# Gated convolution's input with five block groups and four plain tiles, on unscaled operands, and ACT and DVE in a held order at its head

## The chip, the cores and the metric

The kernel runs on one core of a Trainium2 chip. The metric is the time of one execution on the device in microseconds (us); lower is better. The core's engines are PE (TensorE, matmuls), DVE (VectorE), ACT (ScalarE), POOL (GpSimd) and SP (SyncE); SP and POOL here mostly issue DMAs.

## The reference

A causal decoder trunk of two layers over 512 tokens of width 1024, all in float32. Layer 0 is an attention mixer followed by a gated MLP, layer 1 a gated short convolution followed by another gated MLP. The part that is changed is the first half of layer 1's mixer:

```python
def rms_norm(x, g):
    xf = x.astype(jnp.float32)
    y = xf * lax.rsqrt(jnp.mean(xf * xf, axis=-1, keepdims=True) + EPS)
    return (y * g.astype(jnp.float32)).astype(x.dtype)

def short_conv_mixer(h, norm_g, w_in, conv_w, w_out):
    xn = rms_norm(h, norm_g)
    proj = xn @ w_in
    gate_b = proj[..., :CONV_WIDTH]
    gate_c = proj[..., CONV_WIDTH:2 * CONV_WIDTH]
    u = proj[..., 2 * CONV_WIDTH:]
    y = gate_b * causal_dwconv(gate_c * u, conv_w)
    return y @ w_out
```

`causal_dwconv` is a depthwise convolution over three tokens; `CONV_WIDTH` is 1024, so `proj` has 3072 columns: three parts of eight tiles of 128.

## The kernel before

Activations lie transposed, features on the partitions and the 512 tokens along the row, so the residual `h` is eight tiles of 128x512. TensorE works in a reduced form of float32; every operand is kept as a high half and a low half, and a product of two operands is three matmuls: high by high, low by high, high by low. For weights, the high half `whi` is a rounding copy by ACT, and the low half `wlo` is the difference, by DVE.

A matrix product is done in one of two ways:

- A **plain tile** is 128 output columns by all 512 tokens: 8 blocks of features, three matmuls each, 24 matmuls of 512 columns (`products`, `mm3`, L336 to L338). Its weights come through a list (`want`, `weights`) with `whi` at L315 and `wlo` at L316. The operands are `hs_a` and `hs_b`, the halves of `h` times the norm's gain. They are not scaled by the norm's factor of the token, which comes later and is multiplied onto the result.
- A **block group** (class `Sevens`) is 256 output columns by all 512 tokens, computed as a 2x2 block product (features in two halves, tokens in two halves) with seven products in place of eight. Each product is 24 matmuls of 256 columns (`seven`, L1078). They run in the order p1, p7, p3, p6, p2, q5, q4, one in each slot (`slot(g, s)`), where the slot of p3 does that of the group before. Each product has an operand form, made once for all groups out of the blocks of the operand (a, b the left and right tokens of the first four feature tiles, c, d those of the last four), and weights made for each group: four blocks X, Y, W, Z by DMA, sums of them by accumulating DMAs on POOL's queue (`add_block`) and by DVE (`Y+=X`, L1144; `Y+=W`, L1199), and halves by ACT and DVE (`weights_of`, L1027 and L1029). PSUM bank A gathers p1 and p2, bank T p7 and q4, bank R p3, p6 and q5. R begins as a copy of −A that ACT makes in slot 1 (L1185), and p6 of the same group accumulates into it.

`halves_to` makes a form's halves: `p7_hi` by ACT, then `p7_lo` by DVE.

The gated convolution's input has 24 tiles of output columns. Before, eight are plain (u and gate_c tiles 0 and 1, then gate_b tiles 0 to 3), and sixteen are block groups 1 to 4: groups 1 to 3 hold u and gate_c tiles 2g and 2g+1, group 4 gate_b tiles 4 to 7. The groups' operand is scaled: `prepare` multiplies `h` by gain and norm row into `x0` and `x1` (eight rows of 128x512 on DVE, L1453), then makes the seven forms. The pieces of `prepare`, and of the scaling and convolution of the plain tiles (`input_`, `gate`), are chores that `up.work_off(SHARE)` hands out between the matmuls of the plain tiles.

The norm's factor `norm.row` is made late: squares of `h` (`sq_n`, ACT), sums on PE (L410), thirteen small rows of 128x4 on DVE, a turn on PE (L396), and a copy on ACT (L397). `norm.finish(x)` sets when, and `norm.scaled(f)` puts off `f` until the row is there.

The order of instructions on an engine is the scheduler's, save where the code holds it: `pin(m)` and `behind(m, n)` hold single instructions, and with `strict[0]` set ACT and DVE keep the order in which the code is written. `tail(p, s)` does the elementwise work of a group once its results are there: u times gate_c, the convolution, times gate_b, and the halves `y` for the output product, which begins after the last group (L336 and so on into bank `psa`).

Of the kernel before, what the change touches and what calls it, by code (L numbers as in the profile page):

```python
# [17 lines left out]
F32 = mybir.dt.float32  # L18
# [7 lines left out]
P = 128  # L26
# [24 lines left out]
FAR = 41  # L51
CHUNKS = ((2, 3), (5, 3), (8, 3)), ((0, 3), (3, 4), (7, 4))
EARLY, LATER = 4.0, 5.0
SHARE = 0.58


@with_exitstack
def trunk(
# [967 lines left out]
    def halves_to(hi, lo, src, sign=1.0, held=()):  # L1026
        made = act.activation(hi, src, AF.Copy, scale=sign)  # L1027
        if sign > 0:
            rest = dve.tensor_tensor(lo, src, f32(hi), op=ALU.subtract)  # L1029
        else:  # L1030
            rest = dve.scalar_tensor_tensor(lo, src, -1.0, f32(hi), op0=ALU.mult, op1=ALU.subtract)
        for m, engine in ((made, "act"), (rest, "dve")):
            if engine in held:
                pin(m)

    LEFT, RIGHT = slice(0, HT), slice(HT, S)
    FORMS = ("p1", "p7", "p3", "p6", "p2", "q5", "q4")
# [45 lines left out]
    class Sevens:  # L1083
# [23 lines left out]
        def weights_of(self, g, form, n):  # L1107
            hi, lo = (wp.tile([P, CHUNK], F32R, tag=f"w{t}", name=f"w{t}_{form}{self.name}{g}", bufs=3)[:, 0:1024].rearrange(
                "p (k c) -> p k c", c=2 * P) for t in ("hi", "lo"))
            halves_to(hi, lo, self.st[g][n], held=("act",))  # L1110
            self.st[g][form] = hi, lo

        def bank_of(self, g, n):
# [16 lines left out]

        def join(self, g, n, acc, other):
            to = self.wides[g][n][:, :, RIGHT]
            dve.tensor_tensor(to, acc.rearrange("p (i t) -> p i t", t=HT), other.rearrange("p (i t) -> p i t", t=HT), op=ALU.subtract)
            if self.scaled:
                dve.tensor_tensor(to, to, self.row(RIGHT), op=ALU.mult)

# [231 lines left out]
    def conv_seven(norm, mp, rp):  # L1368

        def block_of(g, kh, half):  # L1370
            c0 = (4 + 2 * half) * P if g == 4 else (2 - half) * D + 2 * g * P
            return conv_w_in[0][kh * 512:(kh + 1) * 512, c0:c0 + 2 * P].rearrange("(k p) c -> p k c", p=P)

        up = Sevens("c", mp, range(1, 5), block_of)
        up.norm, up.chores, up.ahead = norm, [], True
        chores, wides, room = up.chores, up.wides, []

        def eight(dt, name):
            t = rp.tile([P, 8, S], dt, tag="head", name=name)
            return t[:, 0:4, :], t[:, 4:8, :]  # L1380
        early_t, early_b = eight(F32, "early")
        ys = []

        def place(k, n):
            if not room:
                room.append(hsp.tile([P, 12, S], F32, tag="hs_a", name="hs_a_conv"))
            return room[0][:, k:k + n, :]
        up.wides_of = lambda g: {"yg": place(8, 2), "yv": place(10, 2)}

        def conv(o, src):  # L1390
            dst = early_t[:, 2 + o, :] if o < 2 else place(o, 1)[:, 0, :]
            causal_conv(dst, src, lambda i: conv_tap(i, o))

        def halves_in(o, n):
            y_hi, y_lo = ys[o // 4]
            at_ = slice(o % 4, o % 4 + n)
            halves_to(y_hi[:, at_, :], y_lo[:, at_, :], place(o, n))

        def open_ys():
            ys.append((hsp.tile([P, 4, S], F32R, tag="hs_b", name="y_hi1"), rp.tile([P, 4, S], F32R, tag="four", name="y_lo1")) if ys else eight(F32R, "y0"))  # L1400

        def times(o, side, with_):
            t = place(o, 2)[:, :, side]
            dve.tensor_tensor(t, t, with_, op=ALU.mult)

        def by_tile(acc):
            return acc.rearrange("p (i t) -> p i t", t=HT)

        def left(g, acc):
            if g == 4:  # L1410
                times(4, LEFT, by_tile(acc))
            else:
                up.to_wide(g, "yg", LEFT, acc)

        def early(g, acc):
            if g == 4:
                times(6, LEFT, by_tile(acc))
            else:
                u = wides[g]["yg"][:, :, LEFT]
                dve.tensor_tensor(u, u, by_tile(acc), op=ALU.mult)  # L1420
        up.left, up.early = left, early

        def tail(p, s):
            u, c = (wides[p][n] for n in ("yg", "yv"))
            if p == 4:
                if s == 0:
                    open_ys()
                    times(6, RIGHT, c[:, :, RIGHT])
                    times(4, RIGHT, u[:, :, RIGHT])
                    halves_in(4, 2)  # L1430
                elif s == 3:
                    halves_in(6, 2)
            elif s == 0:
                if p == 2:
                    halves_in(2, 2)
            elif s == 1:
                dve.tensor_tensor(u[:, :, RIGHT], u[:, :, RIGHT], c[:, :, RIGHT], op=ALU.mult)
            elif s in (3, 4):
                conv(2 * p + s - 3, u[:, s - 3, :])
            elif s == 5 and p == 1:  # L1440
                dve.tensor_tensor(place(0, 2), early_t[:, 2:4, :], early_b[:, 0:2, :], op=ALU.mult)
                times(2, slice(0, S), early_b[:, 2:4, :])
                open_ys()
            elif s == 6 and p == 1:
                halves_in(0, 2)
        up.tail = tail

        def prepare():
            x0, x1 = mp.tile([P, 4, S], F32, tag="x0", name="x0_prep"), rp.tile([P, 4, S], F32, tag="four", name="x1_prep")
            s0, s1 = (mp.tile([P, 4, HT], F32, tag=t, name=f"{t}_prep", bufs=2) for t in "XY")  # L1450
            for x, f in ((x0, 0), (x1, 4)):
                for i in range(4):
                    dve.scalar_tensor_tensor(x[:, i, :], h[:, f + i, :], gain_of(norm.base, f + i), norm.row, op0=ALU.mult, op1=ALU.mult)  # L1453
                    yield 0.75
            a, b, c, d = x0[:, :, LEFT], x0[:, :, RIGHT], x1[:, :, LEFT], x1[:, :, RIGHT]
            for n, src, made in (("p1", a, None), ("p7", s0, (a, b, ALU.subtract)), ("p6", s0, (s0, d, ALU.add)), ("p2", c, None),
                                 ("q5", s1, (b, d, ALU.subtract)), ("q4", d, None), ("p3", s0, (c, s0, ALU.subtract))):
                if made:
                    dve.tensor_tensor(src, made[0], made[1], op=made[2])
                    yield 1.22  # L1460
                halves_to(*up.forms[n], src)
                yield 1.22

        def input_(o, u, c):
            x, y = early_t[:, 0, :], early_t[:, 1, :]
            for t, acc in ((x, u), (y, c)):
                dve.tensor_tensor(t, acc, norm.row, op=ALU.mult)
                yield 0.69
            dve.tensor_tensor(x, x, y, op=ALU.mult)
            yield 0.69  # L1470
            conv(o, x)
            yield 1.5

        def gate(o, acc):
            dve.tensor_tensor(early_b[:, o, :], acc, norm.row, op=ALU.mult)
            yield 0.69

        accs = []
        for j in range(8):
            accs.append(bank("bbbbaabb"[j]))  # L1480
            for _ in products(accs[-1], weights(), (4, 5, 6, 7, 0, 1, 2, 3)):
                up.work_off(SHARE)
            if j in (1, 3):
                chores.append(input_(j // 2, *accs[j - 1:]))
            if j == 3:
                chores.append(prepare())
            if j >= 4:
                chores.insert(0, gate(j - 4, accs[j]))
            if j == 5:
                up.load_pair(1)  # L1490
                up.add_block(1, "Y", 1, 1)
            if j == 7:
                up.weights_of(1, "p1", "X")
                up.first_sums(1)
                up.weights_of(1, "p6", "Y")
        want_conv_out()
        for s in range(28):
            up.slot(1 + s // 7, s % 7)
            if s == 20:
                sum_far(99)  # L1500
            if s == 27:
# [290 lines left out]
```

## Time and profile before

| | us |
|---|---|
| median of three runs | 1119.33 |
| lowest, highest | 1117.55, 1121.01 |
| the profiled execution's own time | 1119.06 |
| its span, from the first to the last instruction | 1117.3 |
| first matmul of the input's plain tiles | 610.02 |
| first matmul of its block groups | 656.12 |
| first matmuls of the output product | about 736.5 |

The span is what the profile's rows add up to; 1.8 us of the execution's time lie around it. In the rows, a time stands ahead of a duration, then the engine, the line, what is written and read with its shape, and how often; behind it in brackets the idle time ahead and what ended it. A trailing `c` in `p7_hic` or `whi_p6c` is the name of this input's groups; a number behind it in the lists of the order is the group.

### The profile page before, as it was taken

The numbers are of one execution on the slowest core, as the hardware profiler recorded it, in microseconds if no ns is written. First come the engines' busy times: TensorE is split into PE (matmuls) and PEld (weight loads), VectorE is DVE, ScalarE is ACT, GpSimd is POOL, SyncE is SP. The second block draws the span as 40 slices with busy tenths as digits, with TensorE's granted clock in tenths as the row PEclk, the third lists the DMA queues.
The fourth block names the chain that finished last, engine by engine and source line by source line (L and its number), as shares of the span: only waits on it lengthen the run. The fifth ranks groups of instructions, "written<-read, shape, count | busy, mean of one in ns | idle before, by whom it ended". The sixth has DMA issues, their size and how long they took to land.

```text
span 1117.3 us, 19714 instructions
## 1 busy us (share of the span) xinstructions
PE 1109.9 (99%) x7803; PEld 1014.2 (91%) x7803; DVE 960.8 (86%) x1483; ACT 681.2 (61%) x1006; POOL 175.4 (16%) x199
## 2 busy tenths in 40 slices
PE   9999999999999999999999999999999999999998
PEld 7888787878899999999999899988999999998886
DVE  6798888997899787898989888867899999999886
ACT  7466677655466666666557355545666656567553
POOL 4011111111012221014400001110111221014300
PEclk9999999999999999999999999999999999999999
DMA  6668877778678887899963355696879887899951
GB/s 196 169 182 202 199 175 207 190 206 227 177 174 200 204 202 177 218 271 193 226 178 81 113 145 139 138 278 168 214 185 219 195 201 181 218 260 206 231 152 57
DMA packets 176988, 210.94 MB, mean 189 GB/s; under 512 B 7580, under 2 KB 142796, under 8 KB 176896
## 3 DMA queue, kind: packets, MB, share of 16 engines
q0 software_dynamic: 50112, 92.19, 42.7%
q1 hardware_dynamic: 126624, 117.42, 33.4%
q8 instruction: 61, 1.00, 0.3%
q14 instruction: 31, 0.25, 0.1%
q10 hardware_dynamic: 160, 0.07, 0.0%
HBM read 204.68 MB, written 44.04 MB: 223 GB/s over the span
## 4 chain that ended last, share of the span: by engine, by line
PE 96%; DVE 2%; issue 1%; ACT 1%; DVEq 0%; ACTq 0%
PE psb L1078 31%; PE psa L1078 12%; PE psb L1670 11%; PE psa L1670 8%; PE psb L336 6%; PE psb L338 5%; PE psb L337 5%; PE psb L710 2%; PE psa L338 2%; PE psa L337 2%; PE psa L336 2%; PE psa L807 2%; PE psc L782 1%; PE psb L592 1%; PE psb L593 1%; PE psb L594 1%
## 5 line engine op out<-in xcount | busy, mean ns | idle before, releaser
L1078 PE MATMUL psb<-p_hi,whi_p 128*128 128x256 f32 x480 | 135.4, 282 | 0.0
L1078 PE MATMUL psb<-p_lo,whi_p 128*128 128x256 f32 x480 | 135.2, 282 | 0.0
L1078 PE MATMUL psb<-p_hi,wlo_p 128*128 128x256 f32 x480 | 135.0, 282 | 0.0
L315 ACT ACTIVATE whi<-raw 128x1024 fp32r<-128x1024 f32 (+2 forms) x81 | 83.2, 1028 | 80.3 <-PE psb L337 27.8
L316 DVE TENSOR_TENSOR wlo<-raw,whi 128x1024 fp32r<-128x1024 f32 (+2 forms) x81 | 95.8, 1183 | 20.8 <-ACT whi L315 20.2
L1078 PEld LDWEIGHTS psb<-p_hi,whi_p 128*128 128x128 f32 x480 | 91.0, 189 | 0.0
L1078 PEld LDWEIGHTS psb<-p_lo,whi_p 128*128 128x128 f32 x480 | 90.5, 189 | 0.0
L1078 PE MATMUL psa<-p_hi,wlo_p 128*128 128x256 f32 x320 | 90.2, 282 | 0.0
L1078 PE MATMUL psa<-p_lo,whi_p 128*128 128x256 f32 x320 | 90.2, 282 | 0.0
L1078 PE MATMUL psb<-q_lo,whi_q 128*128 128x256 f32 x320 | 90.2, 282 | 0.0
L1078 PE MATMUL psb<-q_hi,whi_q 128*128 128x256 f32 x320 | 90.1, 282 | 0.0
L1078 PEld LDWEIGHTS psb<-p_hi,wlo_p 128*128 128x128 f32 x480 | 90.1, 188 | 0.0
L1078 PE MATMUL psa<-p_hi,whi_p 128*128 128x256 f32 x320 | 90.0, 281 | 0.0
L1078 PE MATMUL psb<-q_hi,wlo_q 128*128 128x256 f32 x320 | 90.0, 282 | 0.0
L336 PE MATMUL psb<-hs_a,whi 128*128 128x512 f32 x192 | 79.3, 413 | 0.0
L338 PE MATMUL psb<-hs_a,wlo 128*128 128x512 f32 x192 | 76.2, 398 | 0.0
L1670 PE MATMUL psb<-act,whi 128*128 128x256 f32 x352 | 63.3, 282 | 0.0
L1078 PEld LDWEIGHTS psa<-p_hi,whi_p 128*128 128x128 f32 x320 | 60.6, 190 | 0.1
L1078 PEld LDWEIGHTS psb<-q_hi,whi_q 128*128 128x128 f32 x320 | 60.6, 189 | 0.0
L1078 PEld LDWEIGHTS psa<-p_lo,whi_p 128*128 128x128 f32 x320 | 60.3, 189 | 0.1
L1078 PEld LDWEIGHTS psb<-q_lo,whi_q 128*128 128x128 f32 x320 | 60.4, 189 | 0.0
L1078 PEld LDWEIGHTS psa<-p_hi,wlo_p 128*128 128x128 f32 x320 | 60.1, 188 | 0.0
(551 smaller groups left out, 3596.7 us busy)
## 6 DMA issues: line engine op xcount, KB each, us to landing
t<-in_ffn_w_up POOLq DMA_DIRECT2D x24, 768.0 KB, 8.0
raw<-in_attn_w_in SPq DMA_DIRECT2D x24, 512.0 KB, 5.0
t<-in_ffn_w_up POOLq DMA_DIRECT2D x12, 1024.0 KB, 10.1
X<-in_ffn_w_up SPq DMA_DIRECT2D x20, 512.0 KB, 5.0
Y<-t SPq DMA_DIRECT2D x20, 512.0 KB, 6.6
three<-t SPq DMA_DIRECT2D x20, 512.0 KB, 5.4
W<-in_ffn_w_up SPq DMA_DIRECT2D x20, 512.0 KB, 4.0
Z<-in_ffn_w_up SPq DMA_DIRECT2D x20, 512.0 KB, 5.5
```

Of the source, the lines that this page charges most:

```text
L315: return (act.activation(hi[:, at_], raw[:, at_], AF.Copy), dve.tensor_tensor(lo[:, at_], raw[:, at_], f32(hi[:, at_]), op=ALU.subtract))
L316: dve.tensor_tensor(lo[:, at_], raw[:, at_], f32(hi[:, at_]), op=ALU.subtract))
L336: made = [pe.matmul(acc, w[0], rhs[0], start=first, stop=False), pe.matmul(acc, w[0], rhs[1], start=False, stop=False), pe.matmul(acc, w[1 ...
L337: pe.matmul(acc, w[0], rhs[1], start=False, stop=False),
L338: pe.matmul(acc, w[1], rhs[0], start=False, stop=last)]
L592: pe.matmul(acc, lhs[0], w[0], start=first, stop=False)
L593: pe.matmul(acc, lhs[0], w[1], start=False, stop=False)
L594: pe.matmul(acc, lhs[1], w[0], start=False, stop=last)
L710: pe.matmul(ss[e][:, c:c + wide], ql[rows, b * P:n], kl[rows, 0:wide], start=first and b == bs[0], stop=last and b == bs[-1])
L807: pe.matmul(out_, w, t[:, first:first + step * (NB - k - 1) + 1:step, :], start=k == 0 and i == 0, stop=k == NB - 1 and i == 1)
L1078: pe.matmul(to, w[a][:, k, c], x[b][:, k, :], start=fresh and i + k + t == 0, stop=i == 1 and k == 3 and t == 2, skip_group_check=not fresh)
L1670: pe.matmul(to, l, r, start=begin and o + t == 0, stop=end and t == 2 and o == (0 if layer else 1), skip_group_check=not fresh)
```

## The change

The input becomes five block groups (0 to 4) and four plain tiles (gate_b 0 to 3). Group 0 holds u and gate_c tiles 0 and 1.

The forms are made from unscaled operands. Eight rows by ACT (`raw.take`, 128x512) write `h` times gain to `x0` and `x1`; p7, p6, q5 and p3 come from these (`raw.make`). p1, p2 and q4 are blocks of `hs_a` and `hs_b` as they are, copied by six DMAs of 512 KB on POOL's queue (`copied`). Since the results then lack the norm's factor, u times gate_c is multiplied by `row2`, the square of the row (slot 3 after each of groups 0 to 3, 128x1024), and gate tiles 4 to 7 by the row (two multiplies of 128x1024, each held behind an instruction named in the code).

From the last `raw.take` to the making of p3 in slot 2 of group 0, `strict[0]` holds ACT and DVE in the order of the code, and the table `plan` says between which matmuls of the plain tiles each piece is written. `SUMS2` sets the sums of this norm later.

```diff
+SUMS2 = 9.0
 def want_conv():
-    for part, o in ((2, 0), (1, 0), (2, 1), (1, 1)) + tuple((0, o) for o in range(4)):
-        want(conv_w_in[0], 0, 8, part * D + o * P, P)
+    for o in range(4):
+        want(conv_w_in[0], 0, 8, o * P, P)
...
-up = Sevens("c", mp, range(1, 5), block_of)
+up = Sevens("c", mp, range(5), block_of)
+row2 = mp.tile([P, S], F32, tag="row2", name="row2")
...
 # tail(p, s): p the group that has just ended
             if p == 4:
                 if s == 0:
                     open_ys()
+                    behind(times(6, slice(0, S), both(norm.row)), up.joined)
...
             elif s == 1:
                 dve.tensor_tensor(u[:, :, RIGHT], u[:, :, RIGHT], c[:, :, RIGHT], op=ALU.mult)
+                if p == 3:
+                    behind(times(4, slice(0, S), both(norm.row)), up.rest)
             elif s in (3, 4):
+                if s == 3:
+                    dve.tensor_tensor(u, u, both(row2), op=ALU.mult)
                 conv(2 * p + s - 3, u[:, s - 3, :])
...
-def prepare():
...
-        for x, f in ((x0, 0), (x1, 4)):
-            for i in range(4):
-                dve.scalar_tensor_tensor(x[:, i, :], h[:, f + i, :], gain_of(norm.base, f + i), norm.row, op0=ALU.mult, op1=ALU.mult)
...
-for j in range(8):
-    accs.append(bank("bbbbaabb"[j]))
-    for _ in products(accs[-1], weights(), (4, 5, 6, 7, 0, 1, 2, 3)):
-        up.work_off(SHARE)
...
+raw = RawForms(up, (x0, x1), ...)
+def copied(name, k0, side):
+    for part, to in enumerate(up.forms[name]):
+        own_, at_ = (hs_now["b"], 0) if part and k0 else (hs_now["a"], 8 if part else k0)
+        pin(nc.gpsimd.dma_start(to, own_[:, at_:at_ + 4, side]))
+def gate(o, acc):
+    norm.scaled(lambda: dve.tensor_tensor(early_b[:, o, :], acc, norm.row, op=ALU.mult))
+def open_first():
+    up.load_pair(0)
+    copied("p1", 0, LEFT)
+    up.add_block(0, "Y", 1, 1)
+    copied("q4", 4, RIGHT)
+copied("p2", 4, LEFT)
+first = weights()
+for f in (0, 1, 4, 5, 2, 3, 6, 7):
+    raw.take(f)
+strict[0] = True
+norm.scaled(lambda: dve.tensor_tensor(row2, norm.row, norm.row, op=ALU.mult))
+accs = [bank("b") for _ in range(4)]
+plan = {
+    (0, 7): open_first, (1, 0): lambda: raw.make("p7"),
+    (2, 1): lambda: up.weights_of(0, "p1", "X"), (2, 2): lambda: raw.make("p6"), (2, 7): lambda: (gate(0, accs[0]), gate(1, accs[1])),
+    (3, 0): lambda: up.first_sums(0), (3, 5): lambda: gate(2, accs[2])}
+for j, acc in enumerate(accs):
+    for k, _ in enumerate(products(acc, weights() if j else first, (4, 5, 6, 7, 0, 1, 2, 3))):
+        if (j, k) in plan:
+            plan[j, k]()
+up.weights_of(0, "p6", "Y")
 want_conv_out()
-for s in range(28):
-    up.slot(1 + s // 7, s % 7)
+for s in range(35):
+    up.slot(s // 7, s % 7)
+    if s == 0:
+        gate(3, accs[3])
+        raw.make("q5")
+    if s == 2:
+        raw.make("p3")
+        strict[0] = False
...
-    after_.finish()
+    after_.finish(SUMS2)
```

How the order moves. On ACT, the rows that lead from the plain tiles to the first group's R bank. Before (`psb252` is the R bank of group 1, `whi89` the last plain weight):

```order
L315 ACTIVATE whi89_7593<-raw89_7595 128x1024
L1027 ACTIVATE p2_hic_7370<-x1_prep_7562 128x1024
L1027 ACTIVATE q4_hic_7374<-x1_prep_7562 128x1024
L1027 ACTIVATE p7_hic_7364<-X_prep_7563 128x1024
L1027 ACTIVATE whi_p1c1_7698<-Xc1_7629 128x1024
L1027 ACTIVATE q5_hic_7372<-Y_prep_7564 128x1024
L1027 ACTIVATE p6_hic_7368<-X_prep_7563 128x1024
L1027 ACTIVATE whi_p7c1_7702<-Yc1_7630 128x1024
L1027 ACTIVATE whi_p6c1_7708<-Yc1_7630 128x1024
L1185 ACTIVATE psb252_7772<-psa250_7714 128x512
L1027 ACTIVATE p3_hic_7366<-X_prep_7563 128x1024
```

And now (`psb248` is the R bank of group 0, `whi85` the last plain weight, and `early` holds the sums a−b, (a−b)+d, b−d):

```order
L75 ACTIVATE whi85_7433<-raw85_7435 128x1024
L75 ACTIVATE p7_hic_7364<-early_7376 128x1024
L75 ACTIVATE whi_p1c0_7503<-Xc0_7424 128x1024
L75 ACTIVATE p6_hic_7368<-early_7376 128x1024
L75 ACTIVATE nrow_n2_7522<-psc245_7523 128x512
L75 ACTIVATE whi_p7c0_7541<-Yc0_7425 128x1024
L75 ACTIVATE whi_p6c0_7569<-Yc0_7425 128x1024
L75 ACTIVATE q5_hic_7372<-early_7376 128x1024
L75 ACTIVATE psb248_7633<-psa246_7573 128x512
L75 ACTIVATE P7sc0_7636<-psb247_7608 128x512
```

The halves p7_hi, p6_hi and q5_hi now each follow a sum by DVE, the norm's row stands between them, and q5_hi stands straight ahead of the R bank's copy; before, three rows lay between the two.

On DVE, the rows around the first group's p7 and p6. Before, ending with wlo_p6 of group 1:

```order
L1459 TENSOR_TENSOR X_prep_7563<-X_prep_7563,x1_prep_7562 128x1024
L1029 TENSOR_TENSOR q4_loc_7375<-x1_prep_7562,q4_hic_7374 128x1024
L1475 TENSOR_TENSOR early_7376<-psb248_7634,nrow_n2_7467 128x512
L1029 TENSOR_TENSOR p6_loc_7369<-X_prep_7563,p6_hic_7368 128x1024
L1029 TENSOR_TENSOR q5_loc_7373<-Y_prep_7564,q5_hic_7372 128x1024
L1029 TENSOR_TENSOR wlo_p1c1_7699<-Xc1_7629,whi_p1c1_7698 128x1024
L1029 TENSOR_TENSOR wlo_p7c1_7703<-Yc1_7630,whi_p7c1_7702 128x1024
L1475 TENSOR_TENSOR early_7376<-psb249_7667,nrow_n2_7467 128x512
L1144 TENSOR_TENSOR Yc1_7630<-Yc1_7630,Xc1_7629 128x1024
L1459 TENSOR_TENSOR X_prep_7563<-x1_prep_7562,X_prep_7563 128x1024
L1441 TENSOR_TENSOR hs_a_conv_7866<-early_7376 128x1024
L1029 TENSOR_TENSOR wlo_p6c1_7709<-Yc1_7630,whi_p6c1_7708 128x1024
```

And now, from wlo_p1 of group 0 to q5_lo:

```order
L75 TENSOR_TENSOR wlo_p1c0_7504<-Xc0_7424,whi_p1c0_7503 128x1024
L75 TENSOR_TENSOR early_7376<-early_7376,x1_raw_7379 128x1024
L75 TENSOR_TENSOR p6_loc_7369<-early_7376,p6_hic_7368 128x1024
L75 TENSOR_TENSOR row2_7377<-nrow_n2_7522 128x512
L75 TENSOR_TENSOR early_7376<-psb240_7396,nrow_n2_7522 128x512
L75 TENSOR_TENSOR early_7376<-psb241_7397,nrow_n2_7522 128x512
L75 TENSOR_TENSOR wlo_p7c0_7542<-Yc0_7425,whi_p7c0_7541 128x1024
L75 TENSOR_TENSOR Yc0_7425<-Yc0_7425,Xc0_7424 128x1024
L75 TENSOR_TENSOR early_7376<-psb242_7398,nrow_n2_7522 128x512
L75 TENSOR_TENSOR wlo_p6c0_7570<-Yc0_7425,whi_p6c0_7569 128x1024
L75 TENSOR_TENSOR early_7376<-psb243_7399,nrow_n2_7522 128x512
L75 TENSOR_TENSOR early_7376<-x0_raw_7378,x1_raw_7379 128x1024
```

Where a gate, the forms and the weights' halves lay apart, four gates and row2 now stand between the weights of p1, p7 and p6, and p6's form between p1's and p7's weights.

On DVE, behind wlo_p6 of the last group. Before:

```order
L1029 TENSOR_TENSOR wlo_p6c4_8431<-Yc4_8168,whi_p6c4_8430 128x1024
L1199 TENSOR_TENSOR Yc4_8168<-Yc4_8168,Wc4_8401 128x1024
L1029 TENSOR_TENSOR wlo_p2c4_8462<-Wc4_8401,whi_p2c4_8461 128x1024
L1420 TENSOR_TENSOR hs_a_conv_7866<-hs_a_conv_7866,psb258_8198 128x2x256
L1029 TENSOR_TENSOR wlo_q5c4_8492<-Xc4_8167,whi_q5c4_8491 128x1024
L446 SCALAR_TENSOR_TENSOR hs_a_conv_7866<-hs_a_conv_7866,gains_114 128x511 x2
```

And now:

```order
L1030 TENSOR_TENSOR wlo_p6c4_8525<-Yc4_8261,whi_p6c4_8524 128x1024
L1407 TENSOR_TENSOR hs_a_conv_7730<-hs_a_conv_7730,nrow_n2_7522 128x1024
L1202 TENSOR_TENSOR Yc4_8261<-Yc4_8261,Wc4_8495 128x1024
L1030 TENSOR_TENSOR wlo_p2c4_8557<-Wc4_8495,whi_p2c4_8556 128x1024
L1426 TENSOR_TENSOR hs_a_conv_7730<-hs_a_conv_7730,psb257_8291 128x2x256
L1030 TENSOR_TENSOR wlo_q5c4_8587<-Xc4_8260,whi_q5c4_8586 128x1024
L1449 TENSOR_TENSOR hs_a_conv_7730<-hs_a_conv_7730,row2_7377 128x1024
```

The multiply of the gate pair by the row stands behind wlo_p6, and that of group 3's u times gate_c by row2 behind wlo_q5.

On POOL's queue of DMAs, at the head. Before:

```order
L1105 DMA Yc1_7630<-in_conv_w_in 128x4x256
L1105 DMA Xc1_7629<-in_conv_w_in 128x4x256
L1105 DMA Yc2_7742<-in_conv_w_in 128x4x256
L1105 DMA Xc2_7741<-in_conv_w_in 128x4x256
L1105 DMA Yc3_7936<-in_conv_w_in 128x4x256
```

And now:

```order
L1465 DMA p2_hic_7370<-hs_a1_7201 128x4x256
L1465 DMA p2_loc_7371<-hs_b1_7202 128x4x256
L1465 DMA p1_hic_7362<-hs_a1_7201 128x4x256
L1465 DMA p1_loc_7363<-hs_a1_7201 128x4x256
L1107 DMA Yc0_7425<-in_conv_w_in 128x4x256
L1465 DMA q4_hic_7374<-hs_a1_7201 128x4x256
L1465 DMA q4_loc_7375<-hs_b1_7202 128x4x256
L1107 DMA Xc0_7424<-in_conv_w_in 128x4x256
```

The six copies stand ahead of and between the sums for Y and X of group 0.

More of the change, by code (lines that the diff above doesn't have):

```diff
@@ L1034, in halves_to @@
                 pin(m)
+        return rest
     LEFT, RIGHT = slice(0, HT), slice(HT, S)
@@ L1109, in weights_of @@
                 "p (k c) -> p k c", c=2 * P) for t in ("hi", "lo"))
-            halves_to(hi, lo, self.st[g][n], held=("act",))
+            self.rest = halves_to(hi, lo, self.st[g][n], held=("act",))
             self.st[g][form] = hi, lo
@@ L1132, in join @@
             to = self.wides[g][n][:, :, RIGHT]
-            dve.tensor_tensor(to, acc.rearrange("p (i t) -> p i t", t=HT), other.rearrange("p (i t) -> p i t", t=HT), op=ALU.subtract)
+            self.joined = dve.tensor_tensor(
+                to, acc.rearrange("p (i t) -> p i t", t=HT), other.rearrange("p (i t) -> p i t", t=HT), op=ALU.subtract)
             if self.scaled:
@@ L1390, in conv @@
         def conv(o, src):
-            dst = early_t[:, 2 + o, :] if o < 2 else place(o, 1)[:, 0, :]
-            causal_conv(dst, src, lambda i: conv_tap(i, o))
+            causal_conv(place(o, 1)[:, 0, :], src, lambda i: conv_tap(i, o))
         def halves_in(o, n):
@@ L1437, in tail @@
                 dve.tensor_tensor(u[:, :, RIGHT], u[:, :, RIGHT], c[:, :, RIGHT], op=ALU.mult)
+                if p == 3:
+                    behind(times(4, slice(0, S), both(norm.row)), up.rest)
             elif s in (3, 4):
+                if s == 3:
+                    dve.tensor_tensor(u, u, both(row2), op=ALU.mult)
                 conv(2 * p + s - 3, u[:, s - 3, :])
[L1440 to L1443, printed above, removed]
+            elif s == 5 and p < 2:
+                times(2 * p, slice(0, S), early_b[:, 2 * p:2 * p + 2, :])
+                if p == 1:
+                    open_ys()
             elif s == 6 and p == 1:
@@ L1464, in input_ @@
[L1464 to L1472, printed above, removed]
-        def gate(o, acc):
-            dve.tensor_tensor(early_b[:, o, :], acc, norm.row, op=ALU.mult)
-            yield 0.69
-        accs = []
-        for j in range(8):
-            accs.append(bank("bbbbaabb"[j]))
-            for _ in products(accs[-1], weights(), (4, 5, 6, 7, 0, 1, 2, 3)):
-                up.work_off(SHARE)
[L1483 to L1495, printed above, removed]
@@ L1496, in conv_seven @@
-        want_conv_out()
-        for s in range(28):
-            up.slot(1 + s // 7, s % 7)
-            if s == 20:
+        x0, x1 = mp.tile([P, 4, S], F32, tag="x0", name="x0_raw"), rp.tile([P, 4, S], F32, tag="four", name="x1_raw")
+        raw = RawForms(up, (x0, x1), *(early_t[:, k:k + 2, :].rearrange("p i (j t) -> p (i j) t", t=HT) for k in (0, 2)))
+        def copied(name, k0, side):
+            for part, to in enumerate(up.forms[name]):
+                own_, at_ = (hs_now["b"], 0) if part and k0 else (hs_now["a"], 8 if part else k0)
+                pin(nc.gpsimd.dma_start(to, own_[:, at_:at_ + 4, side]))
```

18 lines of the change are left out of this document (5 added, 13 removed).

## The prediction

> **What bounds the kernel now.** I read the page's first parts, then the chain of waits, and then the windows and rows of the stretch that the change rewrites.
>
> ```profile
> span 1117.3 us, 19714 instructions
> PE 1109.9 (99%) x7803; PEld 1014.2 (91%) x7803; DVE 960.8 (86%) x1483; ACT 681.2 (61%) x1006; POOL 175.4 (16%) x199
> PEclk9999999999999999999999999999999999999999
> PE 96%; DVE 2%; issue 1%; ACT 1%; DVEq 0%; ACTq 0%
> PE psc L858 <- DVE blank L129: 1.0, 1, 1.0
> ```
>
> PE is busy 99% of the span at the full granted clock, and 96% of the chain that ends last is PE. The last row, of the table of waits, is PE's longest wait: 1.0 us. So time can be won only by giving PE less work, and is lost wherever DVE or ACT, at 86% and 61% on average, come later than PE. The stretch itself:
>
> ```profile
> 610.02:656.12 46.10, 46.10 (x207) 37.28 (x206) 42.43 (x62) 21.06 (x26) 0.00 (x0) 1.00 0.37 110
> 656.12:736.68 80.56, 80.56 (x675) 80.08 (x674) 69.31 (x73) 44.28 (x53) 12.03 (x11) 1.00 0.70 163
> 700.00:737.00 37.00, 37.00 (x309) 36.58 (x308) 31.63 (x36) 19.44 (x24) 4.27 (x5) 1.00 0.77 175
> 619.56 0.79 PE psc L410 x8
> 625.12 0.45 PE psc L396 x4
> 656.28 2.85 PE psa L1078 x24
> 727.93 8.52 PE psb L1078 x72
> ```
>
> The windows (sum; busy time of PE, weight load, DVE, ACT, POOL; clock; DMA) are the eight plain tiles, the four block groups, and the last 37 us of the groups. PE never stops in them. DVE is 42.43 of 46.10 busy beside the plain tiles: that is where the operand forms of the products are made.
>
> **PE's work.** Of the 46.10 us, 0.79 are the norm's sums and 0.45 the turning of its column into a row; the rest is 44.86 / 8 = 5.61 a tile. A product takes 2.85, a group of seven 19.95. Four tiles fewer and one group more: −22.4 + 19.95 = **−2.5 us**. That is 0.22% and all that the change can win.
>
> **The head: 22.4 us less cover.** Before, the forms were made beside eight tiles. Now PE starts the first product at 610.02 + 4 × 5.61 + 1.24 = 633.7, the second (p7) at 636.55, and wants the third (p6) at 639.4, in the clock of the trace of before. The vector engines' durations:
>
> ```profile
> 612.26 1.04 ACT L315 ACTIVATE whi<-raw 128x1024 fp32r<-128x1024 f32 x1
> 615.14 0.72 ACT L372 ACTIVATE hs_a<-h,gains 128x512 fp32r<-128x512 f32 x1 [1.84 <-DVE h L1606]
> 616.91 0.62 ACT L381 ACTIVATE sq_n<-h 128x512 f32<-128x512 f32 x1
> 644.65 1.06 ACT L1027 ACTIVATE p_hic<-X_prep 128x1024 fp32r<-128x1024 f32 x1 [0.26 <-DVE X_prep L1459]
> 659.22 0.58 ACT L1185 ACTIVATE psb<-psa 128x512 f32<-128x512 f32 x1
> 642.26 1.22 DVE L1029 TENSOR_TENSOR p_loc<-x_prep,p_hic 128x1024 fp32r<-128x1024 f32 x1
> 643.40 1.22 DVE L1459 TENSOR_TENSOR X_prep<-x_prep 128x1024 f32<-128x1024 f32 x1
> 626.23 1.29 DVE L1467 TENSOR_TENSOR early<-psb,nrow_n 128x512 f32<-128x512 f32 x2 [1.37 <-ACT nrow_n L397]
> 622.08 0.16 DVE L430 TENSOR_TENSOR ra_n<-rg_n 128x4 f32<-128x4 f32 x1
> ...
> 623.45 0.16 DVE L432 TENSOR_TENSOR rb_n<-ra_n,rh_n 128x4 f32<-128x4 f32 x1
> ```
>
> So a 128x1024 row is 1.0 on ACT (1.04 to 1.06), and on DVE 1.22 to its result with the next one 1.14 later; a 128x512 row is about 0.6 on either; the norm's small rows stand 0.2 apart (eight in 1.37).
>
> ACT has done the plain weight whi84 at 613.3. Then eight raw rows are new (a scaled copy of 128x512, as L381 is: 0.62 each, 5.0 in all), four behind whi84 and four behind the norm rows hs and sq of the last two tiles (2.4): 613.3 + 2.5 + 2.4 + 2.5 = 620.7. They replace DVE's eight L1453 rows. whi85 ends at 621.7. From here ACT and DVE hold program order and hand rows to each other, and nearly every row waits for its forerunner:
>
> - DVE wlo85 622.9, a−b 624.1; ACT p7_hi 625.1; DVE p7_lo 626.3, the thirteen small rows of the norm, moved here by its later sums (2.6) 628.9, wlo_p1 630.0, (a−b)+d 631.3; ACT p6_hi 632.3; DVE p6_lo 633.5, row2 and two gates (1.8) 635.3, wlo_p7 636.5, just in time for p7.
> - DVE Y+=X 637.7; ACT whi_p6 638.7; DVE wlo_p6 639.9, a gate 640.5, b−d 641.7; ACT q5_hi 642.7; and only then, since q5_hi stands ahead of it, the copy of −A into the R bank, 643.3.
>
> p6 accumulates into that bank. PE wants it at 639.4: **+3.9 us**.
>
> - p6 then runs to 646.2 and p2 to 649.0. ACT meanwhile: P7s and whi_p2 644.9; DVE q5_lo, wlo_p2 646.1, Y+=W 647.2, c−s 648.4; ACT p3_hi 649.4, whi_q5 650.4; DVE wlo_q5 651.8 behind p3_lo. q5's third matmul wants it a quarter of a microsecond after 649.0: **+2.5 us**.
>
> Together 6.4. The held order ends here; group 1's rows lie free from then on.
>
> **The late groups.** Added to DVE in each of groups 0 to 3 is a row2 multiply, and for gate tiles 4 to 7 two row multiplies: each 128x1024, 1.14.
>
> ```profile
> 704.70 1.06 ACT L1027 ACTIVATE whi_q5c<-Xc 128x1024 fp32r<-128x1024 f32 x1 [4.00 <-DMA Xc<-in_conv_w_in]
> 705.80 1.23 DVE L1029 TENSOR_TENSOR wlo_q5c<-Xc,whi_q5c 128x1024 fp32r<-128x1024 f32 x1 [2.61 <-ACT whi_q5c L1027]
> 736.19 1.23 DVE L1029 TENSOR_TENSOR y_lo<-hs_a_conv,y_hi 128x1024 fp32r<-128x1024 f32 x1
> 736.68 0.24 PE psa L337
> ```
>
> Through the middle groups they go into DVE's idle time, of which the four groups have 80.56 − 69.31 = 11.2. In the last two groups idle is 37.00 − 31.63 = 5.4, and 2.6 of it is the one wait for whi_q5, which waits for a DMA; a row that stands behind wlo_q5 can't use it. So 2.8 take up 4 × 1.14 = 4.6: **+1.7 us**. The bounds are 0 (that wait shifts and all fits) and 4.6 (nothing fits); the plain difference is nearer to how full DVE is (85%). At the output, y_lo is done at 737.4; PE's fifth k there comes 2.8 after 736.68, 2.1 later than that, so the multiply of the last gate pair ahead of it (1.14) stays covered: 0. The conv of tiles 0 and 1 and input scaling that went from the head cost PE nothing before and win nothing now.
>
> **The copies.** Six DMAs of 512 KB on POOL's queue, from SBUF to SBUF, now make the forms p1, p2, q4.
>
> ```profile
> head_blocks<-head_blocks POOLq DMA_DIRECT2D x6, 256.0 KB, 7.4
> hs_b_blocks<-hs_b_blocks POOLq DMA_DIRECT2D x4, 128.0 KB, 6.7
> Yc<-in_conv_w_in POOLq DMA_DIRECT2D x4, 512.0 KB, 9.0
> ```
>
> From 6.7 at 128 KB and 7.4 at 256 KB (0.7 for 128 KB more) I estimate 8.8 at 512 KB, much as the load with accumulation takes, and 2.8 from one landing to the next. p1_hi is issued when the last hs rows are there, near 618: it lands by 626.8, p1_lo by 629.6, and the sum for Y, behind them in the queue, by 632.4. They are wanted at 633.7 and (by whi_p7) 634.3: cost 0. If the landings stood twice as far apart, 5.6, Y would come at 638.0, 3.7 late. So the range for this term is 0 to +3.7; it can't gain, as PE waited for nothing there before. SP's loads of group 0 take the place of four plain weights, and wait for no buffer that is late: 0. The Trainium skill, "DMA: Bandwidth & Descriptors", section "Anatomy of one DMA — SWDGE (gpsimd) path", gives 2.0 us and bytes by 436 KB per us, by which a copy would be an estimated 3.2 us and the term 0 for certain. The 9.0 measured here speaks against that size, and the measurement decides.
>
> **Sum.** −2.5 + 3.9 + 2.5 + 1.7 = +5.6. The profiled execution took 1119.06 (span 1117.3 and 1.8 around it), 0.3 under the median of the three runs, 1119.33; so 1124.7 for it, and **1124.9** by the median.
>
> **Rivals.**
> - *The head's chain is shorter.* It is 30 us of handing over from whi85 on, summed with every hand-over in full. If it is 2.5 shorter, the two waits together are 3.9: +3.1, 1122.4; with late rows hidden as well 1120.7. Against it: a hand-over costs almost nothing beside its rows (whi_q5 ends at 705.76, wlo_q5 starts at 705.80 in the rows above), so there is little air in the sum; for it: the sum takes every row as waiting for the one before.
> - *The head is covered (the other side: not slower).* If wlo_q5 came 6.4 earlier, at 645.4, neither wait exists: −2.5 + 1.7 = −0.8, 1118.5, or 1116.8 with the late rows free. It decides when 5.6 of the chain is saved, for instance if the thirteen small rows (2.6) and the gates (2.4) fell into waits of DVE. Against it: they stand in the held order ahead of rows that are ready.
> - *Copies land late:* +3.7, 1128.6. For it: the accumulating load behind them shares their queue; against it: 1.9 of slack at Y (634.3 − 632.4) even by the slow rows.
> - *PE's clock drops in the gap at p6.* PEclk shows nothing but full clock, but no row shows a gap of 3.9 either. If p6 ran at half speed, that is +2.85, of which the wait for q5 would take back 2.5: +0.4, 1125.3. The Trainium skill, "TensorE: Matmul & The Clock Gate", section "Part 1: The HAM clock gate", says that an idle window of about 3.4 us halves the clock; no run here shows it yet.
>
> **How the numbers follow.** Three tenths of a per cent (3.4 us) is about what a measurement can tell from no change. My sum as it stands 0.58 (1123 to 1127, the late term from 0 to 4.6); the clock 0.08; late copies 0.07; shorter chain 0.18; head covered 0.09. Slower by over 3.4: the first three, 0.73. Same: the shorter chain and two thirds of the covered head, 0.24. Faster: even the whole of PE's saving is below 3.4, so it needs something that I don't see, 0.03. The range runs from 1120.5, the short chain with free late rows, to 1129, the late copies, and leaves out about the covered head and as much above.
>
> **What would show it.** The first product starts near 633.7. PE waits about 3.9 at p6 of group 0, ended by ACT's copy into the R bank, which runs straight behind q5_hi, and about 2.5 at q5, ended by wlo_q5; none at p1 and p7. The thirty-five products take 2.85 each without waits. In groups 3 and 4 PE has waits that sum to about 1.7, for DVE's wlo. The copies take about 9 us each. I am wrong if p6 starts without a wait, if PE's waits are for a DMA, or if PE waits at the plain tiles.

## The result, and the profile after

The changed kernel takes 1125.59 us, the median of six runs (1124.53 to 1126.85), beside 1119.2 for six runs of the kernel before: a ratio of 1.0059 (95% interval 1.0046 to 1.0072). It is slower by 6.4 us. The prediction was 1124.9, slower.

The page of the changed kernel: span and busy time, and the chain that ended last by engine.

```profile
span 1123.5 us, 19899 instructions
PE 1110.4 (99%) x7875; PEld 1018.2 (91%) x7875; DVE 964.5 (86%) x1482; ACT 687.3 (61%) x1018; POOL 182.7 (16%) x207
PE 87%; DVE 5%; issue 3%; ACT 3%; DMA 1%; ACTq 0%; DVEq 0%; POOLq 0%
```

And its waits of PE (in total, times, longest):

```profile
PE psb L1080 <- ACT psb L75: 3.5, 1, 3.5
...
PE psb L1080 <- DVE wlo_q4c L1030: 0.9, 1, 0.9
PE psb L1080 <- DVE hs_a_conv L1135: 0.9, 1, 0.9
...
PE psb L1080 <- ACT whi_q4c L1028: 0.4, 1, 0.4
```

PE was 96% of that chain and is now 87%. DVE and ACT are on it, and the longest wait is PE's for the copy into the R bank. The same stretch by windows, cut at the first plain matmul, the first product, the first product of group 1, and the first matmul of the output product:

```profile
609.77:633.51 23.74, 23.74 (x111) 19.28 (x109) 18.53 (x33) 15.90 (x24) 4.47 (x6) 1.00 1.11 285
633.51:656.90 23.39, 19.44 (x145) 18.82 (x144) 18.52 (x19) 9.99 (x12) 2.62 (x2) 0.93 0.51 113
656.90:742.13 85.23, 83.43 (x698) 82.84 (x697) 75.70 (x81) 44.41 (x54) 12.07 (x11) 1.00 0.65 150
```

The four plain tiles take 23.74 without a wait. The middle row holds six products (p3 has no group to work on), 6 × 2.85 = 17.1 of work in 23.39: 6.3 us lost. The last row holds 29 products, 29 × 2.85 = 82.65 of work in 85.23: 2.6 lost. What happens in the middle row, on ACT, DVE and PE:

```profile
637.18 1.06 ACT L75 ACTIVATE whi_p6c<-Yc 128x1024 fp32r<-128x1024 f32 x1 [4.13 <-DVE Yc L75]
641.26 1.06 ACT L75 ACTIVATE q_hic<-early 128x1024 fp32r<-128x1024 f32 x1 [3.02 <-DVE early L75]
642.23 0.58 ACT L75 ACTIVATE psb<-psa 128x512 f32<-128x512 f32 x1
638.27 1.23 DVE L75 TENSOR_TENSOR wlo_p6c<-Yc,whi_p6c 128x1024 fp32r<-128x1024 f32 x1 [0.61 <-ACT whi_p6c L75]
639.41 0.69 DVE L75 TENSOR_TENSOR early<-psb,nrow_n 128x512 f32<-128x512 f32 x1
640.01 1.22 DVE L75 TENSOR_TENSOR early<-x_raw 128x1024 f32<-128x1024 f32 x1
642.86 0.39 PE L1080 MATMUL psb<-p_hic,whi_p6c 128*128 128x256 f32 x1 [3.51 <-ACT psb L75]
```

ACT stands idle for 3.02 us with the R bank's copy next but one in its queue, since q5_hi ahead of it waits for b−d. The copy's own input, bank A, was complete at 636.5, when p1's last matmul ended. PE would have gone on at 639.21 and starts p6 at 642.86: 3.65 later (the row's 3.51 is the part in which it was idle; the last matmul of p7 runs until 639.36).

After the wait PE runs slow for a while. These windows cut the row above at the steps of the granted clock (the number two from the end):

```profile
639.21:642.86 3.65, 0.14 (x3) 0.00 (x1) 2.53 (x4) 1.60 (x3) 1.03 (x1) 1.00 0.98 150
642.86:643.52 0.66, 0.66 (x5) 0.66 (x6) 0.66 (x1) 0.66 (x2) 0.00 (x0) 1.00 1.21 192
643.52:646.90 3.38, 3.38 (x18) 3.38 (x17) 2.66 (x4) 0.74 (x1) 0.00 (x0) 0.50 0.71 115
```

For 3.4 us the clock is 0.50, so p6 takes 4.5 us and not 2.85. So the case is the prediction's sum with its rival of the clock in it: p6's wait 3.65, p6 1.6 longer, and q5 and q4 together 1.0 longer than their work. The three are the 6.3.

### The profile page after: what moved, and what is told of

Its sections match the earlier page's. It is cut to its first block, busy times and chain, and to the rows that moved or that the text cites. A ratio compares the mean times of both kernels' runs of the same rounds, so it can differ in the third digit from the quotient of the medians.

```text
span 1123.5 us, 19899 instructions
## 1 busy us (share of the span) xinstructions
PE 1110.4 (99%) x7875; PEld 1018.2 (91%) x7875; DVE 964.5 (86%) x1482; ACT 687.3 (61%) x1018; POOL 182.7 (16%) x207
## 4 chain that ended last, share of the span: by engine, by line
PE 87%; DVE 5%; issue 3%; ACT 3%; DMA 1%; ACTq 0%; DVEq 0%; POOLq 0%
PE psb L1080 28%; PE psa L1080 11%; PE psb L1672 10%; PE psa L1672 8%; PE psb L337 5%; PE psb L339 4%; PE psb L338 4%; PE psb L711 2%; PE psa L808 2%; PE psa L339 1%; PE psa L338 1%; PE psa L337 1%; DMA Xc<-in_conv_w_in 1%; PE psc L783 1%; PE psb L593 1%
## 5 line engine op out<-in xcount | busy, mean ns | idle before, releaser
L316 ACT ACTIVATE whi<-raw 128x1024 fp32r<-128x1024 f32 (+2 forms) x76 | 77.9, 1026 | 68.5 <-PE psb L338 22.2
L317 DVE TENSOR_TENSOR wlo<-raw,whi 128x1024 fp32r<-128x1024 f32 (+2 forms) x76 | 89.7, 1181 | 22.2 <-ACT whi L316 21.7
L337 PE MATMUL psb<-hs_a,whi 128*128 128x512 f32 x176 | 73.0, 416 | 0.0
L339 PE MATMUL psb<-hs_a,wlo 128*128 128x512 f32 x176 | 70.1, 398 | 0.0
```

Of the source, the lines that this page charges most:

```text
L316: return (act.activation(hi[:, at_], raw[:, at_], AF.Copy), dve.tensor_tensor(lo[:, at_], raw[:, at_], f32(hi[:, at_]), op=ALU.subtract))
L317: dve.tensor_tensor(lo[:, at_], raw[:, at_], f32(hi[:, at_]), op=ALU.subtract))
L337: made = [pe.matmul(acc, w[0], rhs[0], start=first, stop=False), pe.matmul(acc, w[0], rhs[1], start=False, stop=False), pe.matmul(acc, w[1 ...
L339: pe.matmul(acc, w[1], rhs[0], start=False, stop=last)]
```

## The experiments

Two theories stood against each other for the head. By the first, the held order makes the loss: rows that could run stand behind rows that wait. By the second, the head simply has more work for ACT and DVE than four tiles cover. For the late groups: too little idle time on DVE, or a row in the wrong place, or X's DMA. All ratios below are to the kernel before, on the same chip; runs 1 to 4 were timed on one chip and runs 5 to 8 on another, so across the two sets the ratios compare better than the medians.

**1. q5's form behind the R copy.**

```diff
             if s == 0:
                 gate(3, accs[3])
+            if s == 1:
                 raw.make("q5")
```

> q5's form is made behind slot 1 instead of slot 0, so the copy into the R bank no longer stands behind q5_hi on ACT. Theory (the hand-over chain up to wlo_q5 decides, the R copy only sets where PE waits for it): the wait at p6 falls from 3.5 to under 1 us, p2 then waits for its weights (their halves now stand behind q5's), q5 still waits, and the sum of the head's waits stays near 6: 1125.1 us, half a microsecond less than the changed kernel's 1125.6; no wait is long, and the granted clock stays at 1.00. Rival (the R copy's place is the loss itself, and q5's chain has slack behind it): the 3.6 of the wait and the 1.6 of the slow clock are gone: 1120.4.

1126.34 us, ratio 1.0061 (1.0047 to 1.0075). PE's waits now:

```profile
PE psb L1080 <- ACT whi_q5c L1028: 1.4, 1, 1.4
PE psa L1080 <- ACT whi_p2c L75: 1.4, 1, 1.4
PE psb L1080 <- DVE wlo_q4c L1030: 1.2, 1, 1.2
...
PE psa L1080 <- DVE wlo_p2c L75: 0.8, 1, 0.8
```

And the window in which its clock is low:

```profile
649.96:653.38 3.42, 3.42 (x17) 3.42 (x18) 2.05 (x2) 0.71 (x1) 0.00 (x0) 0.50 0.71 204
```

The long wait is gone and the time isn't: PE waits at p2 and at q5 instead. That is the theory's main point, and it excludes the rival's 1120.4. One thing of the expectation missed: the clock fell here too, after waits of which none is over 1.5. The head takes 24.16 and so loses 24.16 − 17.1 = 7.1, about 1.7 of it in the low stretch (half of 3.42) and 5.4 in waits.

**2. ACT and DVE not held.** Same instructions, same data.

```diff
-        strict[0] = True
         norm.scaled(lambda: dve.tensor_tensor(row2, norm.row, norm.row, op=ALU.mult))
```

> The same instructions, but ACT and DVE are never held in the order of the code: the scheduler orders them as before the change. Theory (the head's loss is the held order, by which rows that are ready stand behind rows that wait): p6 starts without the long wait, with about 1 for wlo_p6, and 1.2 at q5; head waits 2.8 in place of 6.3 to 6.8, so about 1121.5 us, 4 less than the changed kernel. Rival (the head has too much work for four tiles of cover, in whatever order): waits move to other products and the sum falls by 1 at most, 1124.6.

1122.86 us, ratio 1.0032 (1.0022 to 1.0043). Its windows, cut at the same events as above:

```profile
608.94:632.69 23.75, 23.75 (x111) 19.25 (x109) 21.91 (x35) 16.64 (x25) 4.46 (x6) 1.00 1.13 286
632.69:652.25 19.56, 18.29 (x145) 17.36 (x144) 14.96 (x16) 9.45 (x12) 2.62 (x2) 1.00 0.61 135
652.25:738.38 86.13, 83.54 (x698) 82.90 (x697) 75.56 (x81) 44.16 (x54) 12.07 (x11) 1.00 0.65 148
```

The head falls to 19.56, that is 2.5 lost in place of 6.3. DVE's column fits the theory: beside the same plain tiles it is busy 21.91 us, and was 18.53 with the order held. These 3.4 us of DVE's work, done beside the plain tiles and not behind them, are nearly the 3.8 that PE wins; that the one makes the other is inferred here from the sizes. The clock stays at 1.00. The expected 1121.5 was 1.4 too low; the head came out as forecast, and the late groups lose 86.13 − 82.65 = 3.5 here.

**3. Without the norm's factor in the groups.** The four row2 multiplies and two row multiplies are left out, so that the output lacks those factors.

```diff
                 if s == 3:
-                    dve.tensor_tensor(u, u, both(row2), op=ALU.mult)
...
-                    behind(times(6, slice(0, S), both(norm.row)), up.joined)
...
-                if p == 3:
-                    behind(times(4, slice(0, S), both(norm.row)), up.rest)
```

> Leaves out the norm's factor in the groups: the four multiplies by row2 and the two multiplies of gate tiles 4 to 7 by the row are not done; the head is untouched. Theory (DVE's added rows make the late waits): the waits of the last group, 0.9 for wlo_q4 and 0.9 for the bank's reader, and the 0.3 at y_lo are gone, 1123.3 us, 2.3 less than the changed kernel. Rival (the last group waits because its X lands late by DMA, and wlo_q5 and wlo_q4 follow from that): at most 0.6 less, 1125.0.

1122.85 us, ratio 1.0036 (1.0023 to 1.0049). The 29 products behind the head, and p6 of group 0:

```profile
657.12:739.78 82.66, 82.66 (x698) 82.66 (x697) 71.87 (x78) 45.63 (x55) 12.07 (x11) 1.00 0.67 155
642.19:647.48 5.29, 5.29 (x24) 5.29 (x25) 4.22 (x4) 1.41 (x2) 0.00 (x0) 0.50 0.70 112
```

PE has no wait at all in these products. So X's DMA does not make the late loss by itself (ACT still waits for it here); without the added multiplies there is none, neither the 2.6 in the groups nor the 0.4 at y_lo (the first pair of output tiles takes 11.14, as before, in place of 11.55). The second row is from the head, which the edit leaves alone: here the clock fell during the gap already and stayed low for 6.8 us, so p6 took 5.3 and not 4.5. Without that this execution's head would have been some 0.8 shorter.

**4. Work in the gap.** 24 matmuls into a bank that nobody reads.

```diff
+            if s == 1:
+                seven(bank("c"), up.st[0]["p1"], up.forms["p1"], True)
```

> A product of 24 matmuls into a bank that nobody reads is put on PE between p7 and p6 of group 0, in the gap of 3.5 us; it is extra work that leaves the result as it is. Theory (p6 was slow, with a granted clock of 0.50, because PE had idled through the gap, and this cost almost nothing since q5 had to wait for its weights anyway): the gap is then under 1 us, p6 takes 2.85 at clock 1.00 in place of 4.5, q5's wait grows by what p6 saves, and the time falls by 0.3 at most, 1125.3. Rival (the slow clock lies on the path): 1.6 less, 1124.0. Rival (the clock fell for another reason than the gap): p6 stays at 4.5 and the time stays.

1125.87 us, ratio 1.0062 (1.0048 to 1.0076). p6, then the 3.4 us ahead of the fall of the clock, then the low stretch:

```profile
642.05:645.01 2.96, 2.96 (x25) 2.96 (x25) 2.24 (x3) 1.40 (x2) 0.00 (x0) 1.00 1.11 175
647.31:650.73 3.42, 1.93 (x11) 1.31 (x11) 2.62 (x3) 3.42 (x5) 0.00 (x0) 1.00 0.43 140
650.73:654.13 3.40, 3.40 (x17) 3.40 (x17) 2.01 (x2) 0.67 (x1) 0.00 (x0) 0.50 0.70 199
```

p6 is at full clock, while in the three profiles with the gap (the changed kernel's, run 3's, run 5's) it is slow. So the gap was what slowed it, and the rival of another reason falls. The time did not change: q5 waits for whi_q5 as forecast (it starts 16.4 us after the first product, 16.7 in the changed kernel), and after that wait the clock fell after all, now on q5, which the expectation did not have. A low clock at p6 is paid out of q5's wait, all but those 0.3; at q5 it is paid in full: the head of this profile takes 24.69, 1.3 more than the changed kernel's.

**5. row2 ahead of wlo_q5.** In the last group DVE's row2 multiply stood behind wlo_q5, which waits for X; ACT's whi_q4 stood behind the convolution's first row, which needs row2. The changed kernel's chain of waits there (L1449 is the multiply, L444 the convolution; pieces called issue are left out):

```profile
720.54 7.84 DMA Xc<-in_conv_w_in
728.49 1.07 ACT whi_q5c L1028
729.58 1.23 DVE wlo_q5c L1030
730.81 1.15 DVE hs_a_conv L1449
731.98 0.73 ACT hs_a_conv L444
...
734.19 1.23 DVE wlo_q4c L1030
735.46 2.89 PE psb L1080 x22
```

```diff
                 if s == 3:
-                    dve.tensor_tensor(u, u, both(row2), op=ALU.mult)
+                    behind(up.rest, dve.tensor_tensor(u, u, both(row2), op=ALU.mult))
```

> The changed kernel with one hold more: in each group wlo_q5 of the next group comes behind the multiply by row2 on DVE, not ahead of it. Nothing is added or left out. Theory (the late loss is one of place: row2 stands behind wlo_q5, which waits for a DMA, and ACT's whi_q4 stands behind the convolution that needs row2): the multiply falls into DVE's idle time ahead of wlo_q5, the waits of 0.9 and 0.9 in the last group go, y_lo's 0.4 stays, and the time is 1124.0, 1.6 less than the changed kernel's 1125.6. Rival (DVE has not enough idle time there, wherever the rows stand): the waits move to other halves of the last group, 0.4 less at most, 1125.2.

1124.77 us, ratio 1.0055 (1.0041 to 1.0069). The two rows on DVE in the last group:

```profile
727.95 1.22 DVE L1449 TENSOR_TENSOR hs_a_conv<-hs_a_conv,row 128x1024 f32<-128x1024 f32 x1
730.70 1.23 DVE L1030 TENSOR_TENSOR wlo_q5c<-Xc,whi_q5c 128x1024 fp32r<-128x1024 f32 x1 [1.53 <-ACT whi_q5c L1028]
```

The window of its 29 products:

```profile
658.21:741.23 83.02, 82.88 (x698) 82.71 (x697) 76.07 (x81) 44.29 (x54) 10.95 (x10) 1.00 0.66 151
```

The late loss falls from 2.6 to 0.4 with every multiply still there, and DVE still waits 1.53 behind row2: it was place, not amount. (The kernel before loses 0.4 in its 28 products too.) The medians show 0.8 of these 2.2 and the ratios 0.4, with intervals that overlap. Behind the first pair of output tiles this profile is 1.6 longer than the changed kernel's (371.4 beside 369.8), 0.8 of it a wait for the sums of the next norm; whether the hold causes that was not tested. The times alone would not have settled this; the windows do.

**6. The head in the order of need**, with the hold of run 5. The gates leave the table `plan`, the former lines for gate 3, q5, p3 and the hold are taken out, the weights of q5 are no longer made in their own slot, and ACT and DVE are held for one short piece only:

```diff
         up.weights_of(0, "p6", "Y")
...
+            if s == 0:
+                for o in (0, 1):
+                    gate(o, accs[o])
+                dve.tensor_tensor(raw.s[1], x0[:, :, RIGHT], x1[:, :, RIGHT], op=ALU.subtract)
+            if s == 1:
+                strict[0] = True
+                up.weights_of(0, "p2", "W")
+                halves_to(*up.forms["q5"], raw.s[1])
+                up.weights_of(0, "q5", "X")
+                strict[0] = False
+                for o in (2, 3):
+                    gate(o, accs[o])
+            if s == 4:
+                raw.make("p3")
```

> All the work of the changed kernel, and the hold of row2 ahead of wlo_q5; at the head ACT and DVE are held only for one short piece, in the order in which PE needs the rows: b-d, the copy into the R bank, the weights of p2, q5's halves, the weights of q5; the gates stand just ahead of the banks they free, and p3 is made after q5's weights. Theory (order, not amount of work, made the head's loss): p6 starts without a wait, the head's waits are 1.6 in place of 6.3, the late ones 1.0 and 0.4 at y_lo; with 2.4 of PE's work saved 1119.5, level with the kernel before (1118.9). Rival (the head has too much work for four tiles): the head keeps the 2.5 of the free order, 1121.4 or more.

1119.08 us, twelve runs, ratio 1.0000 (0.9991 to 1.0009).

```profile
609.00:632.75 23.75, 23.75 (x111) 19.27 (x109) 21.54 (x35) 16.63 (x25) 4.47 (x6) 1.00 1.15 286
632.75:651.28 18.53, 17.86 (x145) 17.24 (x144) 14.52 (x16) 9.29 (x12) 2.62 (x2) 1.00 0.63 128
651.28:734.33 83.05, 82.90 (x698) 82.73 (x697) 76.70 (x82) 44.17 (x54) 10.62 (x9) 1.00 0.67 154
```

Head 1.4 lost, late groups 0.4, clock 1.00. All work of the changed kernel is in it, so the loss of 6.4 us was one of order, at two places, and the rival of too much work falls. Which of the moves at the head won how much beyond the free order of run 2 was not separated. The kernel draws level with the one before: against PE's saving of 2.4 still stand the head's 1.4, the 0.4 at y_lo, and 1.2 behind the first pair of output tiles (371.1 beside 369.9 before; 0.8 of it again the wait for the next norm's sums).

**7. As 6, with the row multiply of gate tiles 4 and 5 not held.**

```diff
                 if p == 3:
-                    behind(times(4, slice(0, S), both(norm.row)), up.rest)
+                    times(4, slice(0, S), both(norm.row))
```

> As the run with the head in need order, and the row multiply of gate tiles 4 and 5 is no longer held behind a weight half of the last group: the scheduler may place it. Theory (a row multiply that is free to move finds idle time ahead of the last group): 0.3 to 0.5 less in the last group, 1119.1. Rival (it is one more row ahead of the last group's p1 weights): the same or 0.5 more, 1120.0.

1119.32 us, ratio 1.0004 (0.9995 to 1.0013): no difference from 6 that can be measured. Its profile lacks the wait of 0.8 in the next norm and has one of 0.8 at q5 of the last group.

**8. The forms p1, p2, q4 by ACT and DVE**, without the six copies, in the free order of run 2.

```diff
-        copied("p2", 4, LEFT)
...
-            copied("p1", 0, LEFT)
...
-            copied("q4", 4, RIGHT)
...
-            (0, 7): open_first, (1, 0): lambda: raw.make("p7"),
+            (0, 7): open_first, (1, 0): lambda: (raw.make("p1"), raw.make("p7")),
```

(p2 is then made in slot 1, q4 in slot 2.)

> The changed kernel with ACT and DVE free at the head, as in the free run, but the forms p1, p2 and q4 are made by ACT and DVE from the raw rows, without the six DMA copies: three rows of 128x1024 more on each engine. Theory (the copies keep that work off a DVE that the head is short of): p7 waits by 2 us or more for its weights' low half, and the time is 3.6 over the free run's 1122.9, 1126.5. Rival (those rows would fit into waits of DVE, the copies gain nothing): 1122.9, within 0.5.

1127.92 us, ratio 1.0077 (1.0063 to 1.0092). PE's waits that are new, both at p7:

```profile
PE psb L1080 <- DVE early L1468: 2.1, 1, 2.1
...
PE psb L1080 <- DVE wlo_p7c L1030: 1.2, 1, 1.2
```

The window in which its clock is low:

```profile
638.78:645.60 6.82, 6.17 (x29) 6.17 (x30) 5.38 (x6) 2.21 (x4) 2.59 (x2) 0.50 0.28 39
```

5.1 over run 2 (ratio 1.0077 beside 1.0032). p7 waits 3.3, but the longer wait is for a gate that frees its bank (`early`, L1468) and only the 1.2 is for wlo_p7, the one forecast. The low clock adds about 3.1 (half of the 6.17 in which PE was busy), and the 1.8 that run 2 lost at p7 and p6 falls away. The copies are worth that much in this order, the slow stretch included.

## Why the prediction was right

By its own steps, in spans of the profiled executions (6.2 longer, its last matmul 6.3 later):

- *PE's work*, −2.5: the plain stretch is 23.74 in place of 46.10, and a product without waits 2.85, so −22.36 + 19.95 = −2.4. The kernel before also had 0.4 of small losses in its groups, 80.17 (from 656.12 to 736.29) − 28 × 2.85, which the sum left out.
- *The head*, +3.9 and +2.5: p6 waited 3.65 at the place and for the copy that was named, and q5 and q4 lost 1.0. The rest came as a low clock, 1.6: the rival with a chance of 0.08 happened. It was shorter than the rival had it (1.6 at p6 and not 2.85), and q5's wait gave back nearly all of it, as the rival said; so the head's total of 6.3 stands beside the 6.4 forecast. The Trainium skill, "TensorE: Matmul & The Clock Gate", section "Part 1: The HAM clock gate", has the clock halve after an idle window of about 3.4 us; the trace agrees here: the gap was 3.65, the clock fell to 0.50, and it stayed there for 3.4. The last section has falls with shorter waits.
- *wlo_q5* was forecast for 651.8 and ended at 651.53, and this execution was 0.25 ahead at the plain tiles, so the chain was off by less than 0.1 in thirty. That close it is in part by luck: up to c−s (ended at 647.79) the rows were 0.2 to 0.4 ahead of the sum; then ACT's copy of a bank (`Xsc`, 647.59), which the sum does not have, waited for the slow p6, and p3_hi behind it started at 648.08, 0.3 after its input.
- *The late groups*, +1.7: 2.6 and only in the last group. The sum took DVE's idle time as a stock to be filled; what happened was one row behind a wait, which the quoted row of wlo_q5 had shown, and which run 5 took away. PE's listed waits, 0.9 for wlo_q4 and 0.9 for the reader of a bank, are all in the last group, and only half are for a wlo. Of the four multiplies in the term, the last comes at 740.72, after the last product has started (739.21), and the tail counts it again; with three the sum would have given 3 × 1.14 − 2.8 = 0.6. That 1.7 lies near 2.6 is luck. Nor is 2.6 a fixed price: runs 1, 2, 4 and 8 leave these rows alone and lose 3.7, 3.5, 3.7 and 4.0 there, with a wait of 0.5 to 0.8 for wlo_p1 of the last group besides; why was not tested.
- *The tail*, 0: 0.4 at y_lo. The sum set one multiply of 1.14 against 2.1 of slack; by the rows the slack was 1.9 (PE takes y_lo at 739.31, it was done at 737.42), and y_lo starts 2.06 after the output product's first matmul, where it started 0.10 ahead of it before. The waits of the last group are not the reason: in run 5 they are gone and the 2.06 and the 0.4 are the same. 1.14 of the 2.16 is the multiply; where the other 1.0 comes from was not tested.
- *The copies*, 0: no wait of PE or ACT is for them. The first of the six took 3.4, near the 3.2 that the prediction set aside; the two for p1, behind it in the queue, took 8.6 and 8.7, as the estimate of 8.8 had it, and the two for q4 longer, with time to spare:

```profile
p_loc<-hs_a POOLq DMA_DIRECT2D x1, 512.0 KB, 8.7
q_hic<-hs_a POOLq DMA_DIRECT2D x1, 512.0 KB, 12.8
q_loc<-hs_b POOLq DMA_DIRECT2D x1, 512.0 KB, 13.4
```

The sum, −2.4 + 6.3 + 2.6 + 0.4 less the 0.4 of small waits and 0.25 by which this execution was ahead at its start, gives 6.25. The forecast of 5.6 for the profiled execution is off by 0.6 because its misses, 0.9 in the late groups and 0.4 at y_lo, are in part offset by the small losses of the kernel before and by the earlier start. The head, its main term, was right in the place, the row and the size.

## What to carry to other kernels

Work taken off the busiest engine also takes away the cover of the others: count what they must finish before its next stage, row by row with every hand-over, and compare that with the cover that is left. Where an order is held by hand, look at each row that waits and ask what stands ready behind it; here one multiply behind a DMA's wait cost 2.2 us. A copy of 0.58 us behind a waiting row decided where PE waited, 3.65 us at p6, but moving it alone won nothing. Removing the wait that a profile names may only show the next one on the same chain (run 1), so test the chain and not the wait.

## What was not expected of the hardware

The granted clock fell in pieces of 3.4 us: 3.4 long in the changed kernel and in runs 1, 4 and 5, and 6.8 in runs 3 and 8. It needs no gap of that length: in runs 1 and 4 no single wait was over 1.5. In run 1 PE was busy 1.5 of the 3.42 us ahead of the fall, in run 4 1.9 of 3.42; in run 2 it was busy 2.6 of the 3.42 around its longest wait, and the clock held. The window of run 1:

```profile
646.54:649.96 3.42, 1.53 (x9) 0.91 (x8) 2.58 (x3) 3.42 (x5) 0.00 (x0) 1.00 0.44 142
```

And that of run 2:

```profile
638.60:642.02 3.42, 2.64 (x20) 2.23 (x19) 2.99 (x3) 1.91 (x3) 2.39 (x2) 1.00 0.47 63
```

Where between 1.9 and 2.6 the limit lies, and whether it is one of busy time at all, these runs leave open. In these runs several short waits close together thus cost twice: once as waits, and again as a slow stretch, by estimate up to 1.7 us of lost work (half of 3.4) or, in run 8, about 3.1.
